# One of the four block sums of Wo as an accumulating transfer on GpSimd's queue instead of an addition on VectorE

## The chip, the cores and the metric

The kernel runs on 1 core of one Trainium2 chip. The metric is the device time of one execution in microseconds (us), as the median of several runs.

## The reference

One layer of a pooling mixer, followed by a residual layer norm, for 2048 rows of 1024 columns in fp32:

```python
h = x @ w_in                                  # 2048 x 4096
u, z = h[..., :2048], h[..., 2048:]
# four groups of 512 columns of u; windows 2, 4, 8, 16: mean over the last w rows, minus u
m = einsum('bsgc,gcd->bsgd', m, w_grp).reshape(B, S, 2048) * scale
y = (m * silu(z)) @ w_out                     # w_out is called wo in the kernel, 2048 x 1024
x = layer_norm(2 ** 0.25 * x + y, ln_g, ln_b)
```

## The kernel before

Every fp32 product is made of three TensorE products of rounded parts: `split` (lines 297 to 300) lets ScalarE round an operand to its high part and VectorE subtract that from the operand for the low part, and `mm3` (302 to 309) multiplies high by high, high by low and low by high into one PSUM bank. The window means commute with the group matrices, so these are first folded into the weights (`fold`, 323), which are stored to the scratch tensors `wv`. The large products are done with seven block products instead of eight (the Winograd form of Strassen's scheme). For this the operands are cut in 2 x 2 blocks and sums of the blocks are formed.

The stages: the fold (to about 93 us), the up products of the first half of the rows (`up`, 419, sixteen of them, each for a pair of column blocks p and a kind "z" or "v", to about 398 us), the down products of that half (`down`, 565), and then up and down for the second half. An up product has seven block products of 12 matmuls each, in the order 1, 5, 6, 2, 7, 3, 4 (lines 475 to 488). Its banks are Y, V and X: after product 7 VectorE adds bank X into the result (line 484), and only then may product 4 write into bank X again.

`right_sums(k)` (549 to 562) makes the four sums of the blocks of Wo for one k. It is called eight times, interleaved with the first half's up products as `RIGHT` says. It loads the two tiles u (blocks b11, b12) and v (b21, b22), 512 KB each (line 553), does four VectorE operations in place (556 to 559), each of 128 x 512, and stores both tiles to the scratch tensor `wt` (561, 562). The second sum of v (line 559) needs the first (558), which needs u's first block (556); line 558 also overwrites the block that line 557 reads. The products of `down` load the blocks of `wt` from 420 us on.

All these loads pass through one ring of six tiles, `raws` (line 269). An up product takes four of them (two loaded, two for sums), `right_sums` two. A tile goes to its next user when all its users are done, the store included. The transfers of the kernel are issued on SP's queue in one order. GpSimd has only small work: a memset of 128 x 32 (line 450) and a copy of the same size to or from `halo` (452, 498) for each v product, and the powers in the layer norm (650, 672).

The order of the work is planned in the code by class `Plan`. Each operation has a cost, and a due time is worked backwards from PE's order: an operation that moves data (`size` over 0) is taken to be done `LANDING + size / RATE / 1e3` after its cost, that is 2.0 us and 1.55 us for size 512. The operations are then issued by readiness and due time (`record`, 137 to 229). The framework under it makes the final order of each engine with estimates of its own.

Of the kernel before, what the change touches and what calls it, by code (L numbers as in the profile page):

```python
# [10 lines left out]
OP = mybir.AluOpType  # L11
# [16 lines left out]
B = 512  # L28
# [204 lines left out]
def pool_mixer_kernel(ctx: ExitStack, tc, x, xT, wuT, wz, wg, scale, wo, ln_g, ln_b, out):  # L233
# [9 lines left out]
    nc = tc.nc  # L243
    plan = Plan()
# [37 lines left out]
    def cell(*key):  # L282
        return cells.setdefault(key, Cell())
# [4 lines left out]
    def dve(cols, run, R, W):  # L288
        return plan.add("DVE", DVE_FIX + DVE_COL * cols, run, R, W)
# [4 lines left out]
    def dma(kb, run, R, W):  # L294
        return plan.add("SP", ISSUE, run, R, W, size=kb)
# [253 lines left out]
    def right_sums(k):  # L549
        u, v = raws.take(), raws.take()  # L550
        for a, b in enumerate((u, v)):
            r = (2 * k + a) * P
            dma(512, lambda r=r, b=b: nc.sync.dma_start(b.tile, wo[r:r + P, :].rearrange("p (a b) -> p a b", a=2)),
                [], [b[0], b[1]])
        b11, b12, b21, b22 = (lambda: u.tile[:, 0]), (lambda: u.tile[:, 1]), (lambda: v.tile[:, 0]), (lambda: v.tile[:, 1])
        dve(B, lambda: nc.vector.tensor_sub(b11(), b11(), b12()), [u[0], u[1]], [u[0]])
        dve(B, lambda: nc.vector.tensor_sub(b12(), b22(), b12()), [u[1], v[1]], [u[1]])
        dve(B, lambda: nc.vector.tensor_add(b22(), b22(), b11()), [v[1], u[0]], [v[1]])
        dve(B, lambda: nc.vector.tensor_sub(b21(), b21(), b22()), [v[0], v[1]], [v[0]])

        dma(512, lambda: nc.sync.dma_start(wt_d[k][:, 0:2], u.tile), [u[0], u[1]], [cell("wt", k, 0), cell("wt", k, 1)])
        dma(512, lambda: nc.sync.dma_start(wt_d[k][:, 2:4], v.tile), [v[0], v[1]], [cell("wt", k, 2), cell("wt", k, 3)])
# [192 lines left out]
    for h in range(2):  # L755
        for i, p in enumerate(ORDER):
            for kind in "zv":
                up(h, p, kind)
                if h == 0 and (i, kind) in RIGHT:
                    right_sums(ORDER[RIGHT.index((i, kind))])  # L760
        down(h)
# [47 lines left out]
```

## Time and profile before

| | us |
|---|---|
| median of 3 runs | 1016.37 (1016.34 to 1016.76) |
| the profiled execution | 1016.88 |
| its span, first to last instruction | 1015.1 |
| PE busy in it | 1006.9 (99%) |
| DVE busy in it | 787.8 (78%) |
| ACT busy in it | 409.0 (40%) |
| POOL busy in it | 24.8 (2%) |

PE is TensorE, PEld its weight loads, DVE is VectorE, ACT ScalarE, POOL GpSimd and SP SyncE, which here issues the transfers. Durations in the trace are us unless marked ns, and L558 is line 558 of the kernel.

### The profile page before, as it was taken

Reading aid. Unit: us, or ns where it says so; the run is one execution under the profiler, and the core shown is the slowest. Engines: PE = TensorE matmul, PEld = TensorE weight load, DVE = VectorE, ACT = ScalarE, POOL = GpSimd, SP = SyncE. Lnnn points to the kernel's source line nnn. Section 1 sums busy time; section 2 is a strip of 40 time slices with the busy share of each in tenths; the row PEclk is TensorE's granted clock in tenths of the full one; section 3 lists DMA queues with packets and bytes.
Section 4 is the critical chain, followed back from the end, with each engine's and each line's share of the span. In section 5 each row is a group of like instructions: output and inputs, shape, how many; then the busy total and the mean of one; then the engine's idle time right before and its main releaser. Section 6 shows DMA issues by size and latency. Waiting matters only on the chain.

```text
span 1015.1 us, 12022 instructions
## 1 busy us (share of the span) xinstructions
PE 1006.9 (99%) x4435; PEld 831.4 (82%) x4435; DVE 787.8 (78%) x989; ACT 409.0 (40%) x524; POOL 24.8 (2%) x45
## 2 busy tenths in 40 slices
PE   9999999999999999999999999999999999999997
PEld 7888888888888888888888888888888888888885
DVE  5578597888988865788789986887985765575897
ACT  5565433433343433455533433433433433343620
POOL 0000000000000000000001100000000000000011
PEclk9999999999999999999999999999999999999999
DMA  9896443326445754986773423313322354966823
GB/s 323 289 329 206 161 154 114 127 71 228 164 174 215 258 204 135 345 262 215 251 255 125 176 88 102 129 56 125 134 104 75 128 205 148 340 227 194 280 107 124
DMA packets 80650, 186.39 MB, mean 184 GB/s; under 512 B 8400, under 2 KB 16976, under 8 KB 80592
## 3 DMA queue, kind: packets, MB, share of 16 engines
q1 hardware_dynamic: 80592, 185.64, 53.0%
q8 instruction: 34, 0.56, 0.2%
q14 instruction: 24, 0.20, 0.1%
HBM read 131.08 MB, written 54.53 MB: 183 GB/s over the span
## 4 chain that ended last, share of the span: by engine, by line
PE 87%; DMA 6%; DVE 5%; issue 1%; SPq 1%; ACT 0%; DVEq 0%; ACTq 0%
PE acc L306 29%; PE acc L307 29%; PE acc L308 29%; DVE w L300 2%; DMA n<-in_xT 2%; DMA raw<-in_wo 2%; DMA raw<-in_wg 1%; DVE xl L300 1%; DMA n<-in_x 1%; DMA raw<-g 0%; DMA raw<-wt 0%; DVE n L318 0%; DVE n L315 0%; DVE z L636 0%; DVE z L639 0%
## 5 line engine op out<-in xcount | busy, mean ns | idle before, releaser
L300 DVE TENSOR_TENSOR w<-raw,w 128x1024 fp32r<-128x1024 f32 (+1 forms) x254 | 289.4, 1145 | 123.4 <-ACT w L299 122.6
L299 ACT ACTIVATE w<-raw 128x1024 fp32r<-128x1024 f32 (+1 forms) x254 | 250.9, 996 | 280.7 <-PE acc L308 154.6
L306 PE MATMUL acc<-xh,w 128*128 128x512 f32 x896 | 348.8, 389 | 0.0
L307 PE MATMUL acc<-xl,w 128*128 128x512 f32 x896 | 348.6, 389 | 0.0
L308 PE MATMUL acc<-xh,w 128*128 128x512 f32 x896 | 348.6, 389 | 0.0
L306 PEld LDWEIGHTS acc<-xh,w 128*128 128x128 f32 x896 | 168.2, 188 | 35.8 <-ACT v L469 0.6
L308 PEld LDWEIGHTS acc<-xh,w 128*128 128x128 f32 x896 | 168.2, 188 | 34.9
L307 PEld LDWEIGHTS acc<-xl,w 128*128 128x128 f32 x896 | 168.2, 188 | 34.8
L306 PE MATMUL acc<-w 128*128 128x512 f32 x400 | 155.7, 389 | 0.1
L308 PE MATMUL acc<-w 128*128 128x512 f32 x400 | 155.6, 389 | 0.0
L307 PE MATMUL acc<-w 128*128 128x512 f32 x400 | 155.6, 389 | 0.0
L306 PEld LDWEIGHTS acc<-w 128*128 128x128 f32 x400 | 75.1, 188 | 16.2 <-DVE n L636 0.5
L308 PEld LDWEIGHTS acc<-w 128*128 128x128 f32 x400 | 75.1, 188 | 15.7
L307 PEld LDWEIGHTS acc<-w 128*128 128x128 f32 x400 | 75.1, 188 | 15.3
L469 ACT ACTIVATE z<-acc 128x512 f32<-128x512 f32 x64 | 38.2, 596 | 98.5 <-PE acc L308 98.4
L469 ACT ACTIVATE v<-acc 128x512 f32<-128x512 f32 x64 | 37.2, 594 | 75.6 <-PE acc L308 61.7
L518 DVE TENSOR_TENSOR n<-n 128x1024 f32<-128x1024 f32 (+3 forms) x48 | 58.6, 1221 | 0.1
L299 ACT ACTIVATE xh<-n 128x256 fp32r<-128x256 f32 (+2 forms) x48 | 33.6, 702 | 50.7 <-DMA n<-in_xT 34.0
L307 PE MATMUL acc<-w,w 128*128 128x512 f32 x128 | 50.2, 392 | 0.1
L306 PE MATMUL acc<-w,w 128*128 128x512 f32 x128 | 50.3, 393 | 0.0
L308 PE MATMUL acc<-w,w 128*128 128x512 f32 x128 | 49.8, 389 | 0.0
L472 DVE TENSOR_TENSOR v<-v,acc 128x512 f32<-128x512 f32 x32 | 22.0, 687 | 34.5 <-PE acc L308 34.5
(101 smaller groups left out, 727.6 us busy)
## 6 DMA issues: line engine op xcount, KB each, us to landing
raw<-g SPq DMA_DIRECT2D x112, 256.0 KB, 4.0
raw<-in_wz SPq DMA_DIRECT2D x32, 512.0 KB, 3.4
raw<-wv SPq DMA_DIRECT2D x32, 512.0 KB, 4.4
g<-v SPq DMA_DIRECT2D x32, 512.0 KB, 3.7
raw<-wt SPq DMA_DIRECT2D x64, 256.0 KB, 4.2
raw<-in_wo SPq DMA_DIRECT2D x48, 256.0 KB, 4.6
raw<-in_wuT SPq DMA_DIRECT2D x32, 256.0 KB, 5.6
n<-in_xT SPq DMA_DIRECT2D x32, 256.0 KB, 5.1
```

The source lines that it names most:

```text
L299: act(cols, lambda: nc.scalar.activation(hi(), src(), AF.Copy), R, H)
L300: dve(cols, lambda: nc.vector.tensor_sub(lo(), src(), f32(hi())), [*R, *H], L)
L306: nc.tensor.matmul(acc, ah, bh, start=first, stop=False, skip_group_check=True)
L307: nc.tensor.matmul(acc, ah, bl, start=False, stop=False, skip_group_check=True)
L308: nc.tensor.matmul(acc, al, bh, start=False, stop=last, skip_group_check=True)
L469: act(B, lambda: nc.scalar.activation(dest(c, half), acc[b].tile, func), [acc[b]["d"]], [me[c, half]])
L472: dve(B, lambda: nc.vector.tensor_add(dest(c, half), dest(c, half), acc[b].tile), [acc[b]["d"], me[c, half]], [me[c, half]])
L518: nc.vector.tensor_add(n.tile[:, lo:], a[:, lo:], a[:, lo - d:OFF + HS - d])
```

## The change

Line 558, the addition of block b11 into block b22 (128 x 512 fp32, 256 KB), is no longer a VectorE instruction. It becomes a transfer from SBUF to SBUF that adds to its destination, issued on GpSimd's queue. To the plan it is an operation of GpSimd with a cost of 1.5 and a size of 512. What it reads and writes, and so what it waits for and what waits for it, stays as it was.

```diff
@@ right_sums(k)
         dve(B, lambda: nc.vector.tensor_sub(b11(), b11(), b12()), [u[0], u[1]], [u[0]])
         dve(B, lambda: nc.vector.tensor_sub(b12(), b22(), b12()), [u[1], v[1]], [u[1]])
-        dve(B, lambda: nc.vector.tensor_add(b22(), b22(), b11()), [v[1], u[0]], [v[1]])
+        plan.add("POOL", 1.5, lambda: nc.gpsimd.dma_start(b22(), b11(), accum_op=OP.add), [v[1], u[0]], [v[1]], size=512)
         dve(B, lambda: nc.vector.tensor_sub(b21(), b21(), b22()), [v[0], v[1]], [v[0]])
```

## Rows read from the trace of the kernel before

**Rows 1.** The page: busy us, share of the span, instructions by engine.

```profile
PE 1006.9 (99%) x4435; PEld 831.4 (82%) x4435; DVE 787.8 (78%) x989; ACT 409.0 (40%) x524; POOL 24.8 (2%) x45
```

**Rows 2.** Stretches: from:to, length, busy us (instructions) by engine, PE clock, DMA.

```profile
250.00:300.00 50.00, 50.00 (x222) 41.17 (x221) 45.89 (x58) 16.95 (x24) 0.34 (x2) 1.00 0.51 179
300.00:350.00 50.00, 50.00 (x223) 41.38 (x222) 44.70 (x59) 19.21 (x26) 0.87 (x3) 1.00 0.58 209
1000.00:1015.10 15.10, 8.14 (x36) 6.39 (x35) 9.19 (x15) 0.00 (x0) 2.00 (x2) 0.93 0.27 104
```

**Rows 3.** PE in order of time: start us, duration us, line, operation.

```profile
5.06 0.80 PE L306 MATMUL acc<-w,w 128*128 128x512 f32 x1
...
278.87 0.39 PE L308 MATMUL acc<-xh,w 128*128 128x512 f32 x1
...
279.55 0.39 PE L308 MATMUL acc<-xh,w 128*128 128x512 f32 x1
279.82 0.50 PE L306 MATMUL acc<-xh,w 128*128 128x512 f32 x1
280.15 0.39 PE L307 MATMUL acc<-xl,w 128*128 128x512 f32 x1
...
1007.75 0.39 PE L308 MATMUL acc<-w 128*128 128x512 f32 x1
```

**Rows 4.** Waits of PEld after the start: who waited for whom, us, times, longest.

```profile
PEld acc L306 <- ACT v L469: 0.6, 3, 0.3
PEld acc L307 <- DVE w L300: 0.5, 1, 0.5
PEld acc L306 <- DVE n L636: 0.5, 1, 0.5
PEld acc L306 <- DVE z L472: 0.3, 1, 0.3
PEld acc L306 <- ACT w L299: 0.2, 1, 0.2
```

**Rows 5.** Groups by line: shapes, count, busy us, mean ns, idle before.

```profile
L558 DVE TENSOR_TENSOR raw<-raw 128x512 f32<-128x512 f32 x8 | 5.5, 688 | 0.2
```

**Rows 6.** Transfers by line: count, KB each, median us from issue to landing.

```profile
raw<-in_wuT SPq DMA_DIRECT2D x32, 256.0 KB, 5.6
wt<-raw SPq DMA_DIRECT2D x16, 512.0 KB, 4.2
g<-z SPq DMA_DIRECT2D x16, 256.0 KB, 2.0
```

**Rows 7.** POOL in order of time: start us, duration us, operation, idle before.

```profile
288.97 0.21 POOL L498 COPY halo<-v 128x32 f32<-128x32 f32 x1 [11.21 <-ACT v L469]
399.13 1.19 POOL L498 COPY halo<-v 128x32 f32<-128x32 f32 x1 [23.92 <-ACT v L469]
```

**Rows 8.** DVE in order of time, around four of the eight calls.

```profile
100.64 0.69 DVE L557 TENSOR_TENSOR raw<-raw 128x512 f32<-128x512 f32 x1 [0.49 <-DMA raw<-in_wo]
102.09 0.69 DVE L559 TENSOR_TENSOR raw<-raw 128x512 f32<-128x512 f32 x1
...
131.14 0.68 DVE L557 TENSOR_TENSOR raw<-raw 128x512 f32<-128x512 f32 x1
...
140.06 0.68 DVE L559 TENSOR_TENSOR raw<-raw 128x512 f32<-128x512 f32 x1
...
279.29 0.69 DVE L557 TENSOR_TENSOR raw<-raw 128x512 f32<-128x512 f32 x1 [0.99 <-DMA raw<-in_wo]
280.02 0.69 DVE L558 TENSOR_TENSOR raw<-raw 128x512 f32<-128x512 f32 x1
280.75 0.69 DVE L559 TENSOR_TENSOR raw<-raw 128x512 f32<-128x512 f32 x1
282.93 0.69 DVE L472 TENSOR_TENSOR v<-v,acc 128x512 f32<-128x512 f32 x1 [1.49 <-PE acc L308]
...
346.38 0.68 DVE L557 TENSOR_TENSOR raw<-raw 128x512 f32<-128x512 f32 x1
...
348.30 0.69 DVE L559 TENSOR_TENSOR raw<-raw 128x512 f32<-128x512 f32 x1
```

**Rows 9.** SP's queue in order of time around the call at 280 us.

```profile
281.47 0.32 SPq L562 DMA_DIRECT2D wt<-raw  x1
285.86 1.49 SPq L423 DMA_DIRECT2D raw<-in_wz  x2
```

**Rows 10.** The first use of those loads on DVE.

```profile
299.66 0.69 DVE L434 TENSOR_TENSOR raw<-raw 128x512 f32<-128x512 f32 x1
```

## The prediction, made before the changed kernel was run

> **What bounds the kernel now.** I read the busy shares first. PE is busy for 1006.9 of 1015.1 us, DVE for 787.8, POOL for 24.8 [rows 1]. A share of 99% can still hide a slow engine, so I looked at PE in order of time. Three matmuls of one `mm3` start 0.68 us apart (278.87 to 279.55), so one takes 0.2267 us [rows 3]. The program has 4435 matmuls [rows 1], 19 of them a warm-up in the code, so 4416, which is 1001.0 us at that pace. The first of them starts at 5.06 us and the last ends at about 1008.1 us, 1003.1 us later [rows 3]. So all gaps of PE after its start come to about 2 us, and the recorded waits of its weight loads add up the same way: 0.6 + 0.5 + 0.5 + 0.3 + 0.2 = 2.1 us [rows 4]. The kernel is PE's own work, with 5.06 us ahead of it and 7.0 us behind it (15.10 less 8.14 in the last window [rows 2]: the last layer norm and its stores).
>
> In the stretch where `right_sums` is at work, PE is busy in all 50 us of each window although DVE is busy for 45.9 and 44.7 of them [rows 2]. DVE is the second most loaded engine there, but it is not the one that PE waits for. A faster DVE can give back at most those 2 us of gaps, and of these only some lie in this stretch: the gap of about 0.15 us at 279.8 and its like [rows 3]. The chance of a gain over 0.2% (2.03 us, which is also about what a measurement of this kernel can tell from no change) is close to nothing.
>
> **The change part by part.** *Removed:* eight VectorE additions of 688 ns, 5.5 us of DVE [rows 5]. PE did not wait for any of them, so this is worth 0 at the end. The cover is that PE runs without a stop while DVE works ahead; if DVE were late, the 5.5 us would count.
>
> *Added:* eight transfers within SBUF, 256 KB each, which read two operands and write one. The trace of before has no such transfer, so I bound the time T from the end of line 557 to the landing. From below: a 256 KB store out of SBUF lands 2.0 us after its issue [rows 6]. From above: the slowest kind of 256 KB transfer takes 5.6 us [rows 6], and if reading the destination costs a second pass of the same kind, it is 11.2 us. The nearest row is the 512 KB store out of SBUF, with as many bytes read as here, 4.2 us [rows 6]. GpSimd has to issue it. Its 128 x 32 copies take 0.21 us and, beside a busy DVE, up to 1.19 us [rows 7], so I add 0.8 us. I take T = 5.0 us, with ends 2.0 and 12.4 us (11.2 + 1.19). For a price that no row has, the Trainium skill gives one: its page "DMA: Bandwidth & Descriptors", section "Anatomy of one DMA — SWDGE (gpsimd) path", has about 2.0 us plus bytes over 436 GB/s for a transfer issued from GpSimd. By that estimate 256 KB takes 2.6 us and the sum would be the same, zero. No row here shows it.
>
> *Moved:* line 559 (the subtraction that needs the sum), the store of v behind it, and the release of v's tile. I follow three queues.
>
> DVE works in order, so if line 559 stands at the head before the transfer has landed, everything behind it waits. The work with the least time to spare there is the addition of bank X (line 484, recorded at L472): it follows product 7, product 3 runs meanwhile, and product 4 must not start before it is done. That is 12 matmuls, 2.72 us [rows 3], less 0.69 for the addition and some 0.2 for the signals, so 1.8 us to spare. At the call of 280 us, line 557 ends at 279.98 and line 559 starts 0.77 us later. DVE then idles for 1.49 us before the addition at 282.93 [rows 8]. With the order of before, T may reach 0.77 + 1.49 + 1.8 = 4.1 us there before PE stops. The same sum gives 4.4 us at the first call and 7.0 at the last [rows 8], and 5.5 and 5.7 at two more. At the other three calls line 559 already starts 8 to 19 us after line 557, as at 131.14 and 140.06 [rows 8], and nothing is lost. With T = 5.0 and the old order the loss would be 0.9 + 0.6 = 1.5 us.
>
> But the order won't stay. The plan takes the transfer as done 1.5 + 1.55 + 2.0 = 5.05 us after its start, and puts other ready DVE work ahead of line 559 until then. It also makes line 557 and the loads due about 4.2 us earlier, since their due times are worked back through the transfer. With line 559 placed about 5 us after line 557, PE stops only from T of about 5.05 + 1.49 + 1.8 = 8.3 us. So at T = 5.0 I cost the wait at 0 to 1.5 us, and take 0.
>
> SP's queue: the store of v comes T less 0.8, some 4.2 us, later where it was tight. Behind it stands the next load into v's tile, which waits for that store to land: store at 281.47, load at 285.86 [rows 9]. The queue's head then waits longer. But those loads feed a product whose first sum DVE does at 299.66 [rows 10], some 10 us after the load has landed by the median of 4.2 us. So 4.2 us fit. Where three calls come in a row, two tiles of the ring of six are held this much longer once in 19 us; the slack is as large there.
>
> POOL's queue: the transfer waits there for line 557, and behind it stand the memset and the halo copy. Both have much time: POOL had idled 11.21 us before the copy at 288.97 [rows 7], and the v tile that it reads is written again only in the next v product. I cost this at 0.
>
> *Sum:* 0 from the removed additions, 0 for DVE's wait (up to 1.5), 0 for SP and POOL. The profiled execution of 1016.88 us would stay as it is; it lies 0.5 us over the median of the runs, 1016.37. The forecast goes by the median: 1016.4 us.
>
> **The rivals.** *Line 559 blocks DVE and PE stops (slower).* The place is the addition of bank X. The point from which it decides is T beyond what the order of DVE allows: 4.1 us at the tightest place with the old order, about 8.3 us with an order that believes 5.05. With the old order and T = 6.5 the five places lose 2.4 + 2.1 + 1.0 + 0.8 + 0 = 6.3 us, which gives 1022.7 us. With T = 12.4 and the new order it is about 4 us at up to five places, 20 us, 1036 us. For it: DVE is 90% busy there [rows 2], so nothing is made up quickly. Against it: the order of before has the same kind of wait in it, PE for ACT's copy into v, and it costs 0.6 us in three times, 0.3 at the most [rows 4].
>
> *GpSimd is held up by DVE, so that T is long.* In the trace the same copy takes 0.21 and 1.19 us [rows 7], so about 1 us can come on top of T, 6.0 in place of 5.0: with the old order 1.9 + 1.6 + 0.5 + 0.3 = 4.3 us, 1020.7 us; with the planned order nothing. The Trainium skill has a rule for this: its page "SBUF — State Buffer", section "Who interferes with whom", says that VectorE locks GpSimd out of a shared pair of ports in its two-port modes, and that `tensor_tensor`, which is nearly all that runs here, takes only the read side of it and did not stall such a transfer. That agrees with the small stretch in the trace and would leave T as it is.
>
> *DVE's relief shows.* PE's gaps in this stretch vanish, at most 2 us in all [rows 4] and about 0.3 here: 1016.1 us, not measurable. A gain over 2.03 us would need something at the ends, the 5.06 or 7.0 us, which the change does not touch.
>
> *The new order disturbs something else.* A different order of the queues can last past 398 us, into the down products, whose loads PE waited for 0.5 us at the most [rows 4]. It could cost 1 to 4 us anywhere, some 1018.9 us.
>
> **How the numbers follow.** Forecast (no measurable change, 1015.4 to 1018.3): 0.72. Line 559 blocks DVE, with or without GpSimd held up: 0.19, from 1018.5 to some 1036, about half of it under 1022. Disturbed order: 0.06. Gain over 2 us: 0.03. That makes faster 0.03, same 0.72, slower 0.25. The range reaches from 1015.4 (the gaps filled and a little) to 1021.5, which leaves out about 0.10 above and 0.04 below; the likeliest case alone would be 1015.4 to 1018.3.
>
> **What would show it.** Right: PE has no new gap between 95 and 360 us, and its weight loads wait for no more than 2 us; DVE's busy time falls by about 5.5 us; line 559 starts 3 to 8 us after line 557 ends, with other DVE work between. T can be read from POOL's issue to line 559's release. Wrong: DVE idle before line 559 with the transfer as its releaser for over 3 us, gaps of PE right behind a product 3, or a span of the PE work over 1005 us.

## The result, and the profile after

The changed kernel takes 1030.0 us in the median (1029.05 to 1032.68), the kernel before, on the same chip, 1016.57 (1016.34 to 1016.86). The ratio is 1.0137, with a 95% interval of 1.0125 to 1.0149: slower by 13.4 us, where 1016.4 was forecast and the range ended at 1021.5.

The page and the windows that answer to [rows 1] and [rows 2]: busy us, share and instructions by engine, then stretches with length, PE, PEld, DVE, ACT and POOL busy, PE clock, DMA share and GB/s.

```profile
PE 1010.7 (98%) x4435; PEld 833.2 (81%) x4435; DVE 782.1 (76%) x981; ACT 409.4 (40%) x524; POOL 30.6 (3%) x53
...
250.00:300.00 50.00, 49.99 (x220) 40.77 (x219) 39.43 (x50) 17.77 (x26) 2.16 (x5) 1.00 0.41 142
300.00:350.00 50.00, 45.48 (x192) 36.67 (x190) 41.01 (x52) 16.01 (x22) 2.89 (x5) 0.97 0.74 244
```

DVE lost its eight additions (989 to 981 instructions, 5.7 us less), and it is less busy in both windows. In the second PE issues 192 matmuls instead of 223. So PE stands still while the engine that was relieved is not busier: DVE waits. PE in order of time, at the four places where it stops for over 2 us (start us, duration us, line, operation, idle before and releaser), with two matmuls behind the third:

```profile
111.16 0.50 PE L306 MATMUL acc<-xh,w 128*128 128x512 f32 x1 [2.31 <-DVE z L472]
...
248.03 0.50 PE L306 MATMUL acc<-xh,w 128*128 128x512 f32 x1 [2.43 <-DVE v L472]
...
307.79 0.74 PE L306 MATMUL acc<-xh,w 128*128 128x512 f32 x1 [2.42 <-DVE z L472]
308.33 0.63 PE L307 MATMUL acc<-xl,w 128*128 128x512 f32 x1
308.76 0.63 PE L308 MATMUL acc<-xh,w 128*128 128x512 f32 x1
...
350.78 0.50 PE L306 MATMUL acc<-xh,w 128*128 128x512 f32 x1 [2.87 <-DVE z L472]
```

Each time product 4 waits for the addition of bank X (recorded at L472), the place that the prediction named as the tightest. Taken from start to start against the pace of 0.2267 us, the four stops are 2.47, 2.59, 2.58 and 3.04 us, 10.7 us together. Behind the third and the fourth the matmuls start 0.43 us apart (308.33 to 308.76) instead of 0.23. The windows of these stretches, and one behind the first stop:

```profile
307.70:311.30 3.60, 3.51 (x8) 2.76 (x9) 3.60 (x6) 0.00 (x0) 0.00 (x0) 0.53 0.96 322
...
352.60:355.80 3.20, 3.20 (x9) 2.44 (x9) 3.20 (x5) 1.79 (x3) 0.00 (x0) 0.52 0.76 309
111.00:115.00 4.00, 3.84 (x17) 3.19 (x18) 0.71 (x2) 1.79 (x3) 0.00 (x0) 1.00 0.99 329
```

The granted clock there is 0.53 and 0.52, the lower of its two levels (1.2 against 2.4 GHz); behind the first stop it is 1.00. Some nine and eight matmuls lose 0.2 us each, 3.4 us. All gaps of PE come to 15.4 us, counted in the same way as 1.7 before, and the difference of 13.7 answers to the 13.4 of the result: 10.7 us are stops, 3.4 us the clock behind two of them, and the small gaps of before, 1.7, have become 1.3.

Who waits for whom (us, times, longest), how long the transfer takes (median us from issue to landing), and how long GpSimd is busy with issuing it (ns, least, median, most):

```profile
DVE raw L559 <- DMA raw<-raw: 27.3, 5, 6.8
DVE raw L434 <- DMA raw<-wv: 10.3, 3, 4.9
...
raw<-raw POOLq DMA_DIRECT2D x8, 256.0 KB, 5.5
...
L558 POOL DMA_DIRECT2D raw<-raw x8: 859/868/1031, 101.3 to 359.7; - x8
```

In five of the eight calls DVE stands at line 559 until the sum has landed. DVE at the first call:

```profile
100.02 0.69 DVE L557 TENSOR_TENSOR raw<-raw 128x512 f32<-128x512 f32 x1 [0.69 <-DMA raw<-in_wo]
107.55 0.69 DVE L559 TENSOR_TENSOR raw<-raw 128x512 f32<-128x512 f32 x1 [6.83 <-DMA raw<-raw]
```

Line 559 stands right behind line 557, as with the old order, in which only line 558 lay between them [rows 8]. From the end of 557 (100.71) to the start of 559 it takes T = 6.8 us; the prediction's limit at this call was 4.4, and 6.8 - 4.4 = 2.4 us is the stop at 111.16 (2.47). At the call of 237 us T is 245.55 - 237.38 = 8.2. The limit there is the prediction's 5.5: in the kernel before, line 559 starts 1.8 us behind line 557 at that call, and DVE then idles for 1.5 and 0.4 us. So 8.2 - 5.5 = 2.7, and the stop at 248.03 is 2.59. These two stops are the rival "line 559 blocks DVE", to within some 0.1 us.

The other two come later than any such wait. The chain of waits before the third (start us, us, what), and the row of DVE where it ends:

```profile
278.36 5.53 DMA raw<-raw
...
283.91 0.70 DVE raw L559
...
284.63 0.32 SPq L562
...
285.47 6.81 DMA raw<-wv
...
292.41 0.69 DVE L434 TENSOR_TENSOR raw<-raw 128x512 f32<-128x512 f32 x1 [3.99 <-DMA raw<-wv]
```

The sum lands late, so the store of v (L562) is issued late, the next load of `wv` behind it on SP's queue is issued late, and DVE stands idle at L434, the first use of that load, 8 us after line 559. From 292.41 on DVE has no idle time any more until the addition of bank X at 307.05, which PE has been waiting for since 305.2. Before the fourth stop both kinds of wait come in one:

```profile
325.49 0.69 DVE L559 TENSOR_TENSOR raw<-raw 128x512 f32<-128x512 f32 x1 [5.93 <-DMA raw<-raw]
...
331.47 0.69 DVE L434 TENSOR_TENSOR raw<-raw 128x512 f32<-128x512 f32 x1 [2.96 <-DMA wt<-raw]
...
350.04 0.68 DVE L472 TENSOR_TENSOR z<-z,acc 128x512 f32<-128x512 f32 x1
```

The second of these waits is for a tile: line 434 writes into one that the store of v still reads. DVE is busy without a gap between 331.5 and 350: the 8.9 us lost at 319 to 331 show on PE 20 us later.

### The profile page after: what moved, and what is told of

It is laid out like the page before. It is cut to its first block, busy times and chain, and to the rows that moved or that the text cites. A ratio compares the mean times of both kernels' runs of the same rounds, so it can differ in the third digit from the quotient of the medians.

```text
span 1029.1 us, 12047 instructions
## 1 busy us (share of the span) xinstructions
PE 1010.7 (98%) x4435; PEld 833.2 (81%) x4435; DVE 782.1 (76%) x981; ACT 409.4 (40%) x524; POOL 30.6 (3%) x53
## 4 chain that ended last, share of the span: by engine, by line
PE 84%; DVE 9%; DMA 4%; issue 1%; ACT 0%; SPq 0%; DVEq 0%; POOLq 0%; ACTq 0%
PE acc L306 28%; PE acc L307 28%; PE acc L308 28%; DMA raw<-raw 2%; DVE n L518 2%; DVE w L300 2%; DMA raw<-wv 1%; DVE z L529 1%; DVE n L526 1%; DMA wt<-raw 0%; DVE raw L435 0%; DVE raw L559 0%; DVE z L472 0%; DVE raw L437 0%; DMA raw<-in_wuT 0%
## 5 line engine op out<-in xcount | busy, mean ns | idle before, releaser
L472 DVE TENSOR_TENSOR v<-v,acc 128x512 f32<-128x512 f32 x32 | 22.0, 687 | 28.1 <-PE acc L308 28.1
```

The source lines that it names most:

```text
L472: dve(B, lambda: nc.vector.tensor_add(dest(c, half), dest(c, half), acc[b].tile), [acc[b]["d"], me[c, half]], [me[c, half]])
```

## The experiments

My first theory after this result (theory A) had one way: DVE waits at line 559, at the head of its order, for a sum that is there only 6 us and more after line 557. The rivals were the longer hold of the tiles and the blocked head of SP's queue (B), the transfer itself by its traffic or GpSimd (C), and the new order of the plan alone (D). Runs e1 to e4 were expected with it, and it missed e1 and e3, which came out 7 and 3 us above it. Theory A2, from then on, has a second way: the late sum holds the store and with it the next loads, and DVE waits again, for these. What each kernel gave, as the ratio to the kernel before measured beside it:

| kernel | ratio | 95% interval | us |
|---|---|---|---|
| the change | 1.0137 | 1.0125 to 1.0149 | 1030.0 |
| e2 the plan's new order, addition on DVE | 1.0006 | 0.9996 to 1.0015 | 1016.9 |
| e12 the transfer added, nobody waits | 1.0001 | 0.9992 to 1.0011 | 1016.6 |
| e13 the transfer added, DVE reads it (early) | 1.0008 | 0.9999 to 1.0017 | 1017.0 |
| e14 the transfer added, DVE waits for it | 1.0075 | 1.0055 to 1.0094 | 1023.3 |
| e1 DVE never waits, store still does | 1.0088 | 1.0073 to 1.0103 | 1025.2 |
| e11 as e1, that store on GpSimd's queue | 1.0184 | 1.0170 to 1.0197 | 1035.1 |
| e3 an addition on GpSimd | 1.0053 | 1.0038 to 1.0068 | 1021.6 |
| e5 half of the columns by transfer | 1.0065 | 1.0048 to 1.0081 | 1023.1 |
| e6 the transfer twice | 1.0253 | 1.0237 to 1.0268 | 1042.2 |
| e4 the plan told 7 us | 1.0126 | 1.0111 to 1.0141 | 1029.2 |
| e9 the kernel before with seven raw tiles | 1.0059 | 1.0044 to 1.0075 | 1022.8 |
| e8 the change with seven raw tiles | 1.0234 | 1.0212 to 1.0255 | 1040.1 |
| e7 as e1, seven raw tiles | 1.0106 | 1.0089 to 1.0123 | 1027.6 |
| e10 as e7, store on GpSimd's queue | 1.0336 | 1.0319 to 1.0353 | 1050.2 |

**The plan's new order alone (e2).** The addition goes back to DVE, with the cost and size that the change gave to the plan:

```diff
-        plan.add("POOL", 1.5, lambda: nc.gpsimd.dma_start(b22(), b11(), accum_op=OP.add), ..., size=512)
+        plan.add("DVE", 1.5, lambda: nc.vector.tensor_add(b22(), b22(), b11()), ..., size=512)
```

> The addition is a VectorE instruction again, but the plan is told what it was told of the transfer (cost 1.5, size 512), so the plan's order is about that of the changed kernel, without the transfer. Theory A: 1016 to 1018 us, no gap of PE over 0.5 us behind a product 3. Rival D (the new order of the work itself costs the 14 us): 1024 to 1031.

1.0006, and PE's gaps come to 1.3 us. The earlier due times of the loads and of line 557 cost nothing. DVE's order in this run is near that of the changed kernel, but not the same, so it clears the plan's due times and not every order.

**The transfer with nobody waiting (e12).** The kernel before, with eight transfers of the same size and kind into a tile that nothing reads:

```diff
+    spare = const.tile([P, B], F32, name="spare")
...
         dve(B, lambda: nc.vector.tensor_add(b22(), b22(), b11()), [v[1], u[0]], [v[1]])
+        plan.add("POOL", 1.5, lambda: nc.gpsimd.dma_start(spare, b11(), accum_op=OP.add), [u[0]], [cell("spare")], size=512)
```

> The kernel before (the addition on VectorE), and beside it a transfer of the same kind and size from b11 into a spare tile that nobody reads, issued on GpSimd at the same place of the plan. It has the transfer's traffic and GpSimd's work on it without a wait for it; tile u is held until it has landed. Rival C (traffic, GpSimd's use of SBUF): 1020 to 1030 us. Theory A2 (only waits for it count): 1016 to 1018 us.

1.0001. The traffic, GpSimd's time and whatever the transfer shares with the engines cost nothing here, and no load on SP's queue waits for the transfer. So the loss of the change is somebody waiting for it. The transfer itself can start earlier here (it needs line 556 alone):

```profile
spare<-raw POOLq DMA_DIRECT2D x8, 256.0 KB, 3.3
```

3.3 us in the median (three of the eight took 5.6 to 6.2) against 5.5 in the changed kernel, where it starts later, beside the stores and loads that the call sets off. That these are the reason was not tested.

**DVE's wait, with the stores free (e13 and e14).** To e12 comes a one-column addition on DVE behind line 559 that reads the spare tile. The stores of the sums don't wait for the transfer.

```diff
         dve(B, lambda: nc.vector.tensor_sub(b21(), b21(), b22()), [v[0], v[1]], [v[0]])
+        dve(1, lambda: nc.vector.tensor_add(probe, spare[:, :1], v.tile[:, 0, :1]), [cell("spare"), v[0]], [cell("probe")])
```

> As the one with the spare tile, and after line 559 one VectorE instruction of one column reads the spare tile, so that VectorE waits for the transfer at its head, while the sums and their stores don't wait. It is the first way (VectorE's wait) without most of the second (the late store and loads); tile v is held only until the small read. Theory A2: 1019 to 1026 us, stops of PE behind a product 3 within some 4 us of the end of such a wait. If VectorE's wait alone were the whole: 1028 to 1031. If only the late loads counted: 1016 to 1018.

This missed as a test: the transfer started after line 556 and had landed in all but two calls, where DVE waited 3.3 us in all. 1.0008 says only that a wait of 1.1 or 2.2 us fits under the limits; PE's one stop, 1.4 us at 338.94, has a chain that runs through two loads of Wo and not through the transfer. In e14 the transfer reads b12 instead, so that it starts at line 557's end, as in the changed kernel:

```diff
-        plan.add("POOL", 1.5, lambda: nc.gpsimd.dma_start(spare, b11(), accum_op=OP.add), [u[0]], [cell("spare")], size=512)
+        plan.add("POOL", 1.5, lambda: nc.gpsimd.dma_start(spare, b12(), accum_op=OP.add), [u[1]], [cell("spare")], size=512)
```

> The kernel before with a ninth part added: a 256 KB accumulating transfer of the second top block into a spare tile on GpSimd's queue, which can start only when line 557 has ended, as the transfer of the changed kernel does, and a one-column addition on VectorE right behind line 559 that reads the spare tile, so that VectorE has to wait for the transfer; the stores of the sums wait for nothing new, and what the transfer writes is no part of the result. Theory one (two ways: VectorE stands still at the head of its order, and the sums' stores and the next loads come late): VectorE waits 20 to 30 us in 5 or 6 of the 8 calls, as in the changed kernel, less the 0.7 us of line 559 that now stands ahead of the wait; three or four stops of PE of 1 to 2.5 us right behind such waits and none 20 us later, 1019 to 1026 us. Rival one (VectorE's wait is everything): 1028 to 1031 us. Rival two (only the late stores and loads count): VectorE waits as long, but PE does not stop, 1016 to 1018 us.

DVE waits 20.0 us in four calls, and the time is 1023.3 us in the median of six runs that spread from 1021.1 to 1028.3, 7.2 us more than the kernel before beside it. In the profiled execution (1025.4 us) PE stops at 111.95 (2.29 us), 247.83 (1.60), 362.79 (1.08) and 384.09 (2.08). DVE's wait and those of SP's queue; DVE at the first call; the chain before the last stop (lines stand two to four further down in this kernel: L562 is line 559, L436 is 434, L425 and L427 are 423 and 425, L474 is 472, L555 is 553 and L603 is 599):

```profile
DVE probe L563 <- DMA spare<-raw: 20.0, 4, 6.4
...
SPq L425 <- DMA spare<-raw: 6.8, 3, 3.8
...
SPq L603 <- DMA spare<-raw: 4.5, 1, 4.5
SPq L427 <- DMA spare<-raw: 2.4, 1, 2.4
SPq L555 <- DMA spare<-raw: 2.0, 1, 2.0
...
101.73 0.69 DVE L562 TENSOR_TENSOR raw<-raw 128x512 f32<-128x512 f32 x1
108.83 0.16 DVE L563 TENSOR_TENSOR probe<-spare,raw 128x1 f32<-128x1 f32 x1 [6.40 <-DMA spare<-raw]
...
354.46 5.66 DMA spare<-raw
...
361.03 0.37 SPq L427
...
361.49 7.57 DMA raw<-wv
...
369.18 0.69 DVE raw L436
...
383.44 0.61 DVE z L474
```

Three stops, 5.0 us, stand right behind such a wait, as expected. The fourth, 24 us after the wait ended, I had not expected here: no store waits for the sum, yet a load of `wv` comes late, because the raw tile that it goes into is released by a split that stands behind the waiting DVE. And the edit did not part the two ways as I meant it to: the transfer reads b12, so it holds u's tile, and loads on SP's queue wait for it for 15.7 us in six places, one of them (L603) just ahead of that load of `wv`. So the first way by itself is worth about 5 of the 7 us of stops, and the rest has a part of the second in it. DVE's wait is not the whole.

**DVE never waits (e1).** The second sum of v is built from two subtractions, b21 - b22 - b11, ahead of the transfer, so that only the store of v and what stands behind it wait:

```diff
-        plan.add("POOL", 1.5, lambda: nc.gpsimd.dma_start(b22(), b11(), accum_op=OP.add), ..., size=512)
         dve(B, lambda: nc.vector.tensor_sub(b21(), b21(), b22()), [v[0], v[1]], [v[0]])
+        dve(B, lambda: nc.vector.tensor_sub(b21(), b21(), b11()), [v[0], u[0]], [v[0]])
+        plan.add("POOL", 1.5, lambda: nc.gpsimd.dma_start(b22(), b11(), accum_op=OP.add), ..., size=512)
```

> VectorE takes b22 and then b11 from b21 in two subtractions ahead of the transfer, so that no VectorE instruction waits for the transfer; the transfer still adds b11 into b22, GpSimd still issues it, and tile v is still held until it has landed and been stored. VectorE has the eight instructions back. Theory A (line 559 at the head of VectorE's queue stops PE): the four stops of 2.5 to 3.0 us go, and with them the slow stretches behind two of them: 1015.8 to 1018 us, PE's gaps about 2 us. Rival B (the longer hold of the tiles and the blocked head of SP's queue starve PE): about 1027 to 1031, gaps still near 15 us. Rival C (the transfer's traffic or GpSimd's use of SBUF slows the engines): as B.

1.0088, 8.8 us: two thirds of the loss are there without a single wait at line 559. SP's queue stands for the sum, and DVE for the loads behind it. The waits (us, times, longest), the chain before the stop at 325, and DVE's rows at its end:

```profile
SPq L563 <- DMA raw<-raw: 30.8, 6, 6.4
...
DVE raw L434 <- DMA raw<-wv: 10.6, 2, 6.2
...
312.80 4.80 DMA raw<-raw
...
317.65 0.32 SPq L563
...
318.06 5.43 DMA raw<-wv
...
323.71 0.69 DVE L434 TENSOR_TENSOR raw<-raw 128x512 f32<-128x512 f32 x1 [4.43 <-DMA raw<-wv]
324.32 0.68 DVE L472 TENSOR_TENSOR v<-v,acc 128x512 f32<-128x512 f32 x1
```

Here line 434 stands right ahead of an addition of bank X, and PE stops for 2.4 us at 325.06. e1 and e14 together are 16 us, the change 13.4. They don't add up to it, because the transfer holds u's tile in both; besides, a DVE that waits for the sum may already have waited for part of the load.

**The second way's cause (e11).** In e1's kernel the store of v moves to GpSimd's queue, so that nothing on SP's queue stands for the sum:

```diff
-        dma(512, lambda: nc.sync.dma_start(wt_d[k][:, 2:4], v.tile), ...)
+        plan.add("POOL", 1.0, lambda: nc.gpsimd.dma_start(wt_d[k][:, 2:4], v.tile), ..., size=512)
```

> The kernel of run e1_two_subs (two subtractions in place of the addition, the transfer last, so that VectorE never waits for it; 1025.2 us) with one edit: the store of the lower sums, which waits for the transfer, stands on GpSimd's queue instead of SyncE's, so that no load or store on SyncE's queue stands behind that wait; the raw tile still comes free only when the store has landed. If the loss of that run comes from SyncE's queue standing still: its waits for the sum are gone, line 434's waits for the load of wv fall to those of the kernel before (about 4 us), and the time is 1016 to 1019 us. If it comes from the raw tile that is held longer: the loads of wv stay late, and the time stays at 1023 to 1027 us.

Neither: 1035.1 us, 10 us worse than e1. The profiled execution, 1031.4 us and the fastest of the five, has stops of 3.90 and 5.04 us at 264.87 and 349.08. The store on SP's queue no longer waits, but now the loads themselves do (L423, L425 and L553, the waits of SP's queue: us, times, longest):

```profile
SPq L423 <- DMA wt<-raw: 14.5, 5, 4.7
SPq L423 <- DMA raw<-raw: 10.9, 4, 4.9
SPq L553 <- DMA wt<-raw: 9.4, 2, 6.4
SPq L425 <- DMA wt<-raw: 7.1, 2, 5.9
SPq L425 <- DMA raw<-raw: 4.8, 2, 3.6
SPq L553 <- DMA raw<-raw: 2.5, 1, 2.5
```

They wait for a tile that is still read by the transfer (18.2 us) or by a store (31.0 us), 49 us in all; in e1's kernel the same loads waited 5.1 us, behind a store that waited 30.8. So a held tile is enough to make the loads late: with the store out of the way, they queue for the tile instead, and DVE's wait for `wv` at L434 stays (9.9 us in two places, 10.6 in e1). My sentence that no load would stand behind the sum was wrong, and with it the 1016 to 1019 us. Why the tiles are held for longer than in e1, and so why it costs 10 us more, the run does not show. Nor does it show that SP's blocked head costs nothing: before e1's stop at 325 the head and u's tile, into which the late load goes, come free with the same landing, so its 8.8 us can't be divided between them. The changed kernel has both (SP's queue in order of time; its waits in us, times, longest):

```profile
284.63 0.32 SPq L562 DMA_DIRECT2D wt<-raw  x1
285.04 1.22 SPq L425 DMA_DIRECT2D raw<-wv  x2
...
SPq L562 <- DMA raw<-raw: 17.0, 3, 6.5
SPq L425 <- DMA raw<-raw: 7.1, 2, 3.6
```

The loads before the third stop go out right behind the store of v, which lands only at 287.6, so they don't go into v's tile, and by the semaphores that they wait for they don't go into u's either: there it was the head of the queue, which stands for the sum for 17.0 us in three calls. Before the fourth stop a load of `wv` itself waits 3.6 us for the transfer, and line 434 for v's store: there it was the held tiles.

**More raw tiles (e9, e8, e7, e10), inconclusive.** If the held tile is the cause, a seventh one (`RAW = 7` in place of 6) should give the second way's share back.

> Control: the kernel before with seven tiles in the ring of loads in place of six. PE is never short there, so 1016 to 1017 us under every theory; more would mean that the seventh tile alone disturbs the order.

> The changed kernel with seven tiles in the ring. Line 559 waits on VectorE as before (some 20 to 27 us of VectorE in five places), the late loads are eased. Theory A2: between the two, 1020 to 1027 us. If the longer hold of the tiles were all: 1016 to 1018. If line 559's wait were all: 1028 to 1031.

> The two subtractions ahead of the transfer (VectorE never waits for it) and seven tiles in the ring, so that the loads behind the call take a tile that is free earlier. Theory A2 (two ways into VectorE's queue: line 559's wait, and the late load whose first sum, line 434, then stands at the head): both ways are eased, 1016 to 1020 us, and VectorE's waits of line 434 for a load of wv fall from 10.6 to about 5 us. If SP's head, blocked by the store of v, is what delays the loads and not the tile: little is gained against six tiles, 1022 to 1026.

> As the two subtractions with seven tiles, and the store of v is issued on GpSimd's queue behind the transfer, so that SP's queue never stands behind the transfer. If SP's blocked head is the second way: 1016 to 1018.5 us, and SP has no wait for the transfer. If not: as with the store on SP.

The control decides this: seven tiles cost the kernel before itself 6 us (e9, stops of 1.4 to 1.8 us at 99, 101 and 343), where I had expected nothing. With them the change takes 1040.1, e1's kernel 1027.6, and with the store moved 1050.2. None of them is faster than its counterpart with six. The ring's size also decides which tile meets which load, so the seventh tile moves more than the cause under test, and these runs say nothing for or against the held tile.

**The price of the sum (e3, e5, e6).** An addition on GpSimd itself, on the same operands:

```diff
-        plan.add("POOL", 1.5, lambda: nc.gpsimd.dma_start(b22(), b11(), accum_op=OP.add), ..., size=512)
+        plan.add("POOL", 1.5, lambda: nc.gpsimd.tensor_tensor(b22(), b22(), b11(), op=OP.add), ..., size=512)
```

> The addition is a GpSimd instruction on the tiles (no transfer), with the changed kernel's plan. VectorE still waits for another engine in the same place, but for a shorter time: estimated 1.0 to 3.5 us from the powers and copies of the trace, under the 4.1 us that the tightest place was worked out to bear. Theory A: 1016 to 1018.5 us. Rival D (the order): 1024 to 1031. If GpSimd and VectorE hold each other up, T would be longer than 4 us and VectorE's neighbouring instructions longer than 0.69 us; then 1018 to 1024.

1.0053. The duration in ns (least, median, most), and DVE's waits for it:

```profile
L558 POOL TENSOR_TENSOR raw<-raw x8: 1295/1615/2817, 100.6 to 349.6; 128x512 f32<-128x512 f32 x8
...
DVE raw L559 <- POOL raw L558: 3.8, 3, 1.5
```

With about a quarter of the transfer's time the waits at line 559 fall from 27.3 to 3.8 us, and one stop of 3.2 us is left at 341.46, with the clock at the lower level behind it. Theory A's 1018.5 us at the most was wrong. The chain before the stop begins 27 us earlier, at a load of `wv` that goes out at 314.30 behind the store of v and for which DVE waits 3.69 us at L434: a late load as in the second way, though this kernel has no accumulating transfer. Half of the columns by transfer, the other half by an addition on DVE:

```diff
+        plan.add("POOL", 1.5, lambda: nc.gpsimd.dma_start(b22()[:, :Q], b11()[:, :Q], accum_op=OP.add), ..., size=512)
+        dve(Q, lambda: nc.vector.tensor_add(b22()[:, Q:], b22()[:, Q:], b11()[:, Q:]), ...)
```

> The transfer covers half of the columns (128 x 256, 128 KB), VectorE adds the other half (about 0.42 us each). If the transfer's time is mostly fixed: T falls by less than 1 us, 1025 to 1030 us. If it goes with its size: T falls to about 4.5 us, close to what the tightest place bears, 1018 to 1023.

And the transfer twice in a row (block b11 is added twice, so the sum is another):

```diff
         plan.add("POOL", 1.5, lambda: nc.gpsimd.dma_start(b22(), b11(), accum_op=OP.add), ..., size=512)
+        plan.add("POOL", 1.5, lambda: nc.gpsimd.dma_start(b22(), b11(), accum_op=OP.add), ..., size=512)
```

> The transfer is done twice, the second after the first, so that b11 is added twice (the sums of Wo are not the reference's). T doubles to some 12.5 to 15 us. Theory A2: each of the five places where VectorE waits for it loses about 6.5 us more, some of it hidden: 1050 to 1070 us. If only the first microseconds of the wait or the order counted: under 1040.

Issue to landing, of half the columns and then of each of the two in a row:

```profile
raw<-raw POOLq DMA_DIRECT2D x8, 128.0 KB, 4.9
...
raw<-raw POOLq DMA_DIRECT2D x16, 256.0 KB, 3.6
```

Half the bytes land only 0.6 us sooner, yet the loss falls from 13.4 to 6.6 us, which is neither of the cases that I had set out: the waits at line 559 come to 21.5 us, the stops are 1.3 to 1.9 us, and none is followed by the lower clock. A pair costs 25.7 us, 12 more than one, which is less than the 33 us or more that I expected: each of the two lands in 3.6 us and not 5.5, and line 559's waits came to 25.8 us in six calls, against 27.3 in five with one. Both agree in sign with a loss that grows with the length of the sum beyond a limit.

**Is it the plan's price (e4)?** The prediction had trusted the plan to put work ahead of line 559 for as long as it takes the transfer to be. Told 7 us instead of 5.05, it should have put more:

```diff
-        plan.add("POOL", 1.5, lambda: nc.gpsimd.dma_start(b22(), b11(), accum_op=OP.add), ..., size=512)
+        plan.add("POOL", 7.0, lambda: nc.gpsimd.dma_start(b22(), b11(), accum_op=OP.add), ...)
```

> The changed kernel, but the plan takes the transfer as done 7.25 us after its start, near what was measured (about 6.2 to 7.6), where it had taken 5.05, and no transfer time is put on the plan's bus. If the plan's times decide where line 559 stands on VectorE: 1016 to 1021 us, line 559 starts 7 us or more after line 557 with work between. If the framework's own order overrides the plan: 1025 to 1035, and VectorE idles ahead of line 559 as in the changed kernel (27.3 us in five times).

1.0126, and at the first call DVE still has line 559 directly behind line 557, with a wait of 6.71 us; the waits come to 24.7 us in five calls. At none of the five waits does the price in the plan move line 559 by more than one instruction. The list that the plan makes, worked out from the code, has two splits and two additions between these lines; the order that DVE runs has none. It is the framework under the plan, with its own estimates, that sets it. What estimate it uses is not shown by any run.

## Why the prediction was wrong, point by point

*PE bounds the kernel, its gaps are some 2 us, a gain is out of reach.* Right. Eight additions less on DVE gave nothing back, and PE's own work is what it was: without the gaps the time is the same.

*The removed additions are worth 0, GpSimd's queue 0, traffic 0.* Right; e12 shows the last two at 1.0001, e2 the plan's order at 1.0006. The rival "GpSimd is held up by DVE" is nearly empty: its issue took 0.86 to 1.03 us, against the 0.8 in the sum. The Trainium skill's page "SBUF — State Buffer", section "Who interferes with whom", says that `tensor_tensor` did not stall such a transfer; the trace agrees, with 0.89 us of issue at 278.36 beside two such operations of DVE and 0.86 at 319.55 beside an idle DVE.

*T = 5.0 us.* Mis-sized: the transfer starts some 0.6 us after the end of line 557 (100.71 to 101.3 at the first call) and lands 5.5 us after that in the median, its 0.87 us of issue included, so 6.1 us; at the two calls with a direct stop it is 6.8 and 8.2. The 4.2 us were taken from the store of 512 KB [rows 6]; the upper end (12.4) held it. By the old order's limits T = 6.1 turns the 1.5 us of loss into 2.0 + 1.7 + 0.6 + 0.4 = 4.7.

*"But the order won't stay."* This is the step that failed first. From the plan's 5.05 us I concluded that line 559 would stand about 5 us behind line 557 and that PE would stop only from T of 8.3 us. At the first call nothing stands between them, at the call of 237 us one split, and at the other three waits one to four operations, 3.0 us at the most, and DVE waits at line 559 for 27.3 us in all. The text ahead of the prediction says that the framework makes the final order, and the sum used the plan's as if it were final. With the old order the prediction's own limits give both direct stops to within some 0.1 us (2.4 against 2.47, 2.7 against 2.59), and the absence of one at 283.91: the wait of 3.20 there is under 1.49 + 1.8 = 3.3. At the two calls with direct stops the old order was the measured one, and a forecast with it would have had these 5 us, not the 13.4.

*SP's queue and the held tile at 0 ("4.2 us fit").* This is the step that failed second; e1, where DVE never waits for the sum, has 8.8 us of it. The working took the call at 280 us, where the load's first use stood 10 us behind its landing [rows 10], as the slack of all. But the slack is not a property of the load: the use at L434 came at 299.66 because DVE's order put it there. In the changed kernel's order it stands at DVE's head at 292.41 while the load is still under way, and a landing of 6.8 us, not the median 4.2, met it.

*"A place to stop is right behind a wait."* Not said in these words, but the rival's sum counted only that. Two of four stops come 15 and 19 us after the last wait of the chain that causes them, and 24 and 25 us after the wait at line 559, since DVE, with no idle time in between, carries its delay along to the next addition of bank X.

*The clock.* Not in the sum at all: 3.4 of 13.4 us are matmuls at the lower level behind two of the stops.

*The rival "line 559 blocks DVE"* had the place, the mechanism and 1022.7 us at T = 6.5. That e14 gives 1023.3 is luck: its four stops lie in part at other places than the rival's five and are of other sizes, and one of them has part of the second way in it. Held against the change, the rival lacked the second way and the clock.

Open: how much of the second way is SP's blocked head and how much the held tiles, why e11 holds its tiles longer than e1, what estimate sets the framework's order, and why the transfer takes 3.3 us in one place and 5.5 in another.

## What to carry to other kernels

Here a step moved from an engine with idle time to a transfer was paid by its length, not by its work: ask who stands at the head of an in-order queue when it lands, and use the order that the trace shows, not the one that a planner intends. Follow the late result one step further than its first reader, to the store that waits for it, to what stands behind that store on its queue, to the buffers that the transfer and the store hold and to the loads that need them; the stop may come 20 us later. A transfer of the same kind and size that nobody waits for was free (e12).

## What the runs showed of the hardware

- An accumulating transfer of 256 KB within SBUF landed 3.3 to 5.8 us after its issue in the median of a kernel (e12, e8; 3.6 to 7.6 within the changed kernel). GpSimd was busy with the issue for 0.86 to 1.03 us. At half the bytes it took 4.9 us (e5), as the whole did in e1's kernel. So here most of it did not go with the size.
- GpSimd's own addition of 128 x 512 in fp32 took 1.3 us at the least, 1.6 in the median and 2.8 at the most (e3), where DVE needs 0.69: longer than DVE, but under the transfer.
- The granted clock fell to the lower level behind stops of 2.58 and 3.04 us (0.53 and 0.52 in windows of 3.6 and 3.2 us); behind stops of 2.47 and 2.59 us it did not. In e4's kernel it was at the lower level behind a stop of only 2.16 us (0.51 from 112.0 to 115.4). So the length of the stop alone does not tell whether it falls. Behind the stop at 350.78 the fall came 1.5 us after PE had started again.
